# A weights-stationary last feed-forward part, later turns in the first one, and an expert path written as a loop

## The chip, the cores and the metric

The kernel runs on one core of one Trainium2 chip. The metric is the device time of one execution in microseconds (us); the figure shown for a kernel is the median of its runs. TensorE (PE) multiplies, VectorE (DVE) and ScalarE (ACT) work element-wise, GpSimd (POOL) does small work, SyncE (SP) issues the loads.

## What is computed

Two transformer blocks over 256 tokens of width 1024, all in float32. The first block is: short convolution mixer, SwiGLU feed-forward part of width 2816, latent attention, and a mixture of 8 experts of width 2048 with the top 2 per token. The second block is: two attentions side by side, then a feed-forward part of width 4096 with a squared ReLU. The parts that the change touches:

```python
def swiglu(h, w_gate, w_up, w_down):              # first feed-forward part and each expert
    return (silu(h @ w_gate) * (h @ w_up)) @ w_down

h = rmsnorm_2(x, mlp_norm_g[l])                   # last feed-forward part
u = einsum('bsd,df->bsf', h, w_up[l])
u = square(relu(u))
x = x + einsum('bsf,fd->bsd', u, w_down[l])
```

## The kernel before

**Precision.** Every float32 operand of a big product is split into a high part, which PE can take exactly, and a remainder. A product of two of them is three products on PE: high x high, remainder x high, high x remainder (`mm3`). Weights are split as they arrive (`split`, L105 to L115): ACT casts 128 x 1024 elements to `w_hi` (L113), DVE subtracts to get `w_lo` (L114). There are five buffers of each, and seven of the raw loads.

**Order.** All weights come through one stream, `weight_parts`; `get()` hands out the next split part and has one more part in the making. SP issues the loads of 1 MB in the stream's order. Tiles, semaphores and the order of each engine's instructions come from a framework that plans them when the program is built; an instruction that is not ready in that plan may let later ones pass. `behind` ties a block's instructions behind a given one, and `fence` does so for the weight splits.

**Entering a part.** `Entry` holds the normed tokens for the next part as columns: `enter` adds the result of the part before to `x` (L441), multiplies by the gain (L442), turns four 128 x 128 blocks on PE against the identity (L409), casts the high part on ACT (L410) and subtracts on DVE (L411). The row's scale `rs`, the inverse root of the mean square, is not multiplied in; it is applied to a product's rows. `half` enters the first 128 tokens while the part before still works on the second 128; `finish` enters those, and `proj` calls it after the first half's products.

**A feed-forward part** (`ffn`, L589). The hidden width is cut into chunks of 512. For each chunk `make` gives the features, and `down` multiplies the features of the chunk before into four accumulators (`acc`: two token halves, two halves of the width). In the last part `make` is `squared`: `proj` holds 128 tokens stationary and streams 512 columns of weights, 24 products for each token half; ACT applies Relu with the row scale (L1360), DVE squares (L1361), and `hidden` turns the features into columns (four transposes for each token half, L409), casts (L410) and subtracts (L411), because `down` needs them as its stationary operand. In the first part `make` is `gated`: two `proj`, Silu on ACT (L620), a product on DVE (L623), then `hidden`.

**The general expert path** (`the_rest`, L1002). The experts are worked for up to 128 tokens each. Only if one expert has more than 128 does a branch (L1006) run a body that handles the rest; the count is loaded into a register of each engine (L1005). With these inputs the branch is not taken. The body is written out for 8 experts with 4 chunks each. Behind the branch, the first instruction of PE is L960.

Of the kernel before, what the change touches and what calls it, by code (L numbers as in the profile page):

```python
# [10 lines left out]
F32 = mybir.dt.float32  # L11
# [30 lines left out]
def block_kernel(ctx: ExitStack, tc: tile.TileContext, i, out):  # L42
# [114 lines left out]
    def weight_parts():  # L157
# [45 lines left out]
        yield from up_and_down((i["w_up_2"][0],), i["w_down_2"][0])  # L203
# [137 lines left out]

    def norm(acc=None):

        hi = hts.tile([P, KD, T], F32R, tag="hT_hi", name="hT_hi")
        lo = hts.tile([P, KD, T], F32R, tag="hT_lo", name="hT_lo")
# [68 lines left out]
    class Entry:  # L414
# [5 lines left out]
        def __init__(self):  # L420
            self.h = [hts.tile([P, KD, T], F32R, tag=f"hT_{s}", name=f"hT_{s}") for s in ("hi", "lo")]
# [181 lines left out]
    def hidden(pool, made, width):  # L603
# [8 lines left out]
    with tc.tile_pool(name="parts0", bufs=2) as parts, tc.tile_pool(name="tables", bufs=1) as tp:  # L612
# [3 lines left out]
        def gated(width, first):  # L616
            pg = proj(h, width, entry.finish if first else None)
# [6 lines left out]
            a = hidden(parts, sg, width)  # L624
# [5 lines left out]
            return a  # L630
# [202 lines left out]
    with ExitStack() as moe:  # L833
# [12 lines left out]
        with tc.tile_pool(name="route", bufs=1) as rp:  # L846
# [23 lines left out]
            x_hi, x_lo = (hts.tile([P, KD, T], F32R, tag=f"hT_{s}", name=f"x_{s}") for s in ("hi", "lo"))  # L870
# [131 lines left out]
        def the_rest():  # L1002

            wg_all, wu_all, wd_all = (i[f"moe_w_{n}"][0] for n in ("gate", "up", "down"))
            n_most = nc.values_load(most_i[0:1, 0:1], min_val=0, max_val=T)  # L1005
            with tc.If(n_most > P, label="rest"):  # L1006
# [4 lines left out]
                def streamed(src):  # L1011
# [4 lines left out]
                for e in range(E):  # L1016
                    for t in range(2):
                        nc.vector.tensor_tensor(pick2[:, t], slots[:, P:T], pos[:, t, e : e + 1].to_broadcast([P, P]),
                                                op=OP.is_equal)
                    room = acts.tile([P, 2, D], F32, tag="xn", name="room", bufs=1)  # L1020
                    x2 = room[:, 0].rearrange("p (k s) -> p k s", k=KD)
                    y2 = room[:, 1]
                    b = bank()
                    for t, ts in enumerate(blocks(2)):
                        nc.tensor.transpose(b[:, ts], pick2[:, t], ident)
                    nc.vector.tensor_copy(put2, b[:, :T])
                    b = bank()
                    for t in range(2):
                        mm(b[:, 0:2], pick2[:, t], gate[:, t, e], t == 0, t == 1)
                    nc.vector.tensor_copy(g2, b[:, 0:2])  # L1030
                    for k0 in range(0, KD, 4):
                        v = bank().rearrange("p (k s) -> p k s", k=4)
                        for k in range(4):
                            ks = slice((k0 + k) * P, (k0 + k + 1) * P)
                            for t in range(2):
                                mm(v[:, k], h_hi[:, t, ks].bitcast(F32), pick2[:, t], t == 0, False)
                                mm(v[:, k], h_lo[:, t, ks].bitcast(F32), pick2[:, t], False, t == 1)
                        nc.vector.tensor_copy(x2[:, k0 : k0 + 4], v)
                    yb = [bank("yb") for _ in range(2)]
                    for c, cs in enumerate(blocks(NC, 512)):  # L1040
                        both = []
                        for w_all in (wg_all, wu_all):
                            b = bank()
                            for k, ks in enumerate(blocks(KD)):
                                mm(b, x2[:, k], streamed(w_all[e][ks, cs]), k == 0, k == KD - 1)
                            both.append(b)
                        sg = acts.tile([P, 512], F32, tag="sg", name="sg")
                        nc.scalar.activation(sg, both[0], AF.Silu, scale=g2[:, 1:2])
                        nc.vector.scalar_tensor_tensor(sg, both[1], g2[:, 1:2], sg, op0=OP.mult, op1=OP.mult)
                        bt = bank()  # L1050
                        for fs in blocks(4):
                            nc.tensor.transpose(bt[:, fs], sg[:, fs], ident)
                        a2 = parts.tile([P, 4, P], F32, tag="a_hi", name="a2")
                        nc.vector.tensor_copy(a2, bt.rearrange("p (f s) -> p f s", f=4))
                        for f in range(4):
                            for n, ns in enumerate(blocks(2, 512)):
                                mm(yb[n], a2[:, f], streamed(wd_all[e][c * 512 + f * P : c * 512 + (f + 1) * P, ns]),
                                   c + f == 0, c == NC - 1 and f == 3)
                    for n, ns in enumerate(blocks(2, 512)):
                        nc.vector.tensor_scalar(y2[:, ns], yb[n], g2[:, 0:1], None, op0=OP.mult)  # L1060
                    for t, ts in enumerate(blocks(2)):
                        for ns in blocks(2, 512):
                            b = bank()
                            mm(b, put2[:, ts], y2[:, ns], True, True)
                            nc.vector.tensor_tensor(x[:, t, ns], x[:, t, ns], b, op=OP.add)
# [288 lines left out]
    h, rs = entry.h, entry.rs  # L1354
    with tc.tile_pool(name="parts2", bufs=2) as parts:
        def squared(width, first):
            pu = proj(h, width, entry.finish if first else None)
            r = [acts.tile([P, 512], F32, tag="sg", name="sg") for _ in range(2)]
            for t in range(2):
# [57 lines left out]
```

## Time and profile before

| | |
|---|---|
| median of 3 runs | 1325.47 us (1325.12 to 1325.68) |
| the profiled execution | 1324.65 us, span 1322.9 us from first to last instruction |
| PE, weight loads | 1275.3 us (96% of the span), 1060.9 us (80%) |
| DVE, ACT | 983.5 us (74%), 807.4 us (61%) |
| mean granted TensorE clock | 0.988 of full speed |
| loads | 320.82 MB, 243 GB/s over the span |

Busy time is the sum of the instructions' records. The record of a 512-column product is some 0.39 us long and overlaps the next, so a busy PE can still have room: the start-to-start time is what counts. "Idle before, releaser" names what an instruction had waited for. The last feed-forward part lies from 1127 us to the end, the first one from 108 to 300 us, and the branch of the expert path near 415 us.

### The profile page before, as it was taken

What the parts mean: (1) busy time and instruction counts of PE and PEld (TensorE: products, weight loads), DVE (VectorE), ACT (ScalarE), POOL (GpSimd) and SP (SyncE); (2) the same over time, 40 slices, a digit from 0 to 9 for tenths busy, and PEclk for the clock granted to TensorE, in tenths of its full rate; (3) what the DMA queues carried; (4) which work ended last, traced back from release to release, by engine and by line L of the source; (5) the groups of instructions that cost most, each with busy time, mean ns of one, the idle gap of its engine ahead of it and who ended that gap; (6) DMA issues with size and microseconds to landing.
All of it is one profiled execution on the core that took longest, in us unless ns stands there. A gap on an engine that the chain in (4) does not pass through costs nothing.

```text
span 1322.9 us, 17290 instructions
## 1 busy us (share of the span) xinstructions
PE 1275.3 (96%) x6413; PEld 1060.9 (80%) x6413; DVE 983.5 (74%) x1256; ACT 807.4 (61%) x1106; POOL 82.7 (6%) x111
## 2 busy tenths in 40 slices
PE   6999999999996999999999999999998999899998
PEld 6998778888685788888888887888787986678887
DVE  6665655457856999999998888898887787655553
ACT  5444544446845877778877677777775565544442
POOL 0000201001520000000000000000001331000000
PEclk9999999999997999999999999999998999999999
DMA  9854655736425999989998898999995432455520
GB/s 315 290 177 163 228 176 126 264 112 208 163 65 203 349 364 349 373 316 356 358 357 328 324 344 324 327 342 353 340 333 178 173 100 92 162 181 176 183 95 32
DMA packets 148609, 320.82 MB, mean 243 GB/s; under 512 B 7787, under 2 KB 34438, under 8 KB 148518
## 3 DMA queue, kind: packets, MB, share of 16 engines
q1 hardware_dynamic: 142912, 314.07, 67.3%
q10 hardware_dynamic: 5606, 5.57, 1.9%
q8 instruction: 53, 0.87, 0.3%
q14 instruction: 38, 0.31, 0.1%
HBM read 317.52 MB, written 2.10 MB: 242 GB/s over the span
## 4 chain that ended last, share of the span: by engine, by line
PE 62%; DVE 3%; ACT 2%; POOL 1%; issue 1%; ACTq 0%
PE bank L58 37%; PE yb L58 13%; PE acc L58 8%; DVE w_lo L114 1%; PE bank L1105 1%; PE bank L409 1%; ACT w_hi L113 1%; PE po L58 1%; PE bank L1258 0%; POOL s L1280 0%; ACT s L1274 0%; POOL yq L1177 0%; POOL raq L1164 0%; DVE x_lo L952 0%; DVE mx L1270 0%
## 5 line engine op out<-in xcount | busy, mean ns | idle before, releaser
L114 DVE TENSOR_TENSOR w_lo<-raw,w_hi 128x1024 fp32r<-128x1024 f32 (+2 forms) x600 | 713.0, 1219 | 224.0 <-ACT w_hi L113 208.3
L113 ACT CAST w_hi<-raw 128x1024 fp32r<-128x1024 f32 (+2 forms) x600 | 608.4, 1044 | 297.9 <-PE bank L58 170.7
L58 PE MATMUL bank<-w_hi,x_hi 128*128 128x512 f32 x512 | 202.7, 396 | 0.9 <-ACT w_hi L113 0.9
L58 PE MATMUL bank<-w_lo,x_hi 128*128 128x512 f32 x512 | 201.6, 394 | 1.1 <-DVE w_lo L114 1.1
L58 PE MATMUL bank<-w_hi,x_lo 128*128 128x512 f32 x512 | 200.0, 391 | 0.0
L58 PE MATMUL bank<-w_hi,hT_hi 128*128 128x512 f32 (+1 forms) x464 | 161.8, 358 | 2.5 <-ACT w_hi L113 2.3
L58 PE MATMUL bank<-w_lo,hT_hi 128*128 128x512 f32 (+1 forms) x464 | 159.6, 354 | 1.0 <-DVE w_lo L114 0.9
L58 PE MATMUL bank<-w_hi,hT_lo 128*128 128x512 f32 (+1 forms) x464 | 159.5, 354 | 0.0
L58 PEld LDWEIGHTS bank<-w_lo,x_hi 128*128 128x128 f32 x512 | 96.4, 188 | 25.6 <-DVE w_lo L114 5.4
L58 PEld LDWEIGHTS bank<-w_hi,x_hi 128*128 128x128 f32 x512 | 96.6, 189 | 20.2 <-ACT w_hi L113 1.8
L58 PEld LDWEIGHTS bank<-w_hi,x_lo 128*128 128x128 f32 x512 | 96.5, 189 | 19.5
L58 PEld LDWEIGHTS bank<-w_hi,hT_hi 128*128 128x128 f32 x464 | 89.5, 194 | 15.3 <-ACT w_hi L113 3.4
L58 PE MATMUL yb<-w_hi,a_hi 128*128 128x512 f32 x256 | 101.1, 395 | 0.0
L58 PE MATMUL yb<-w_hi,a_lo 128*128 128x512 f32 x256 | 101.1, 395 | 0.0
L58 PEld LDWEIGHTS bank<-w_lo,hT_hi 128*128 128x128 f32 x464 | 90.0, 194 | 13.1 <-DVE w_lo L114 1.7
L58 PEld LDWEIGHTS bank<-w_hi,hT_lo 128*128 128x128 f32 x464 | 90.0, 194 | 11.4
L58 PE MATMUL yb<-w_lo,a_hi 128*128 128x512 f32 x256 | 96.4, 398 | 0.0
L58 PE MATMUL acc<-w_lo,a_hi 128*128 128x512 f32 x216 | 85.2, 394 | 0.0
L58 PE MATMUL acc<-w_hi,a_lo 128*128 128x512 f32 x216 | 85.1, 394 | 0.0
L58 PE MATMUL acc<-w_hi,a_hi 128*128 128x512 f32 x216 | 84.5, 391 | 0.0
L450 POOL TENSOR_TENSOR rs<-ms,mhalf 128x1 f32<-128x1 f32 x10 | 6.0, 598 | 835.1 <-DVE ms L449 835.1
L58 PEld LDWEIGHTS yb<-w_hi,a_lo 128*128 128x128 f32 x256 | 48.1, 188 | 11.7
(326 smaller groups left out, 1587.9 us busy)
## 6 DMA issues: line engine op xcount, KB each, us to landing
raw<-in_moe_w_gate_dram SPq DMA_DIRECT2D x64, 1024.0 KB, 6.1
raw<-in_moe_w_up_dram SPq DMA_DIRECT2D x64, 1024.0 KB, 6.7
raw<-in_moe_w_down_dram SPq DMA_DIRECT2D x64, 1024.0 KB, 6.0
raw<-in_w_up_dram SPq DMA_DIRECT2D x16, 1024.0 KB, 5.3
raw<-in_w_down_dram SPq DMA_DIRECT2D x16, 1024.0 KB, 5.0
raw<-in_conv_w_in_dram SPq DMA_DIRECT2D x12, 1024.0 KB, 13.3
raw<-in_ffn_w_gate_dram SPq DMA_DIRECT2D x11, 1024.0 KB, 5.1
raw<-in_ffn_w_up_dram SPq DMA_DIRECT2D x11, 1024.0 KB, 18.0
```

The source lines that it names most:

```text
L58: return nc.tensor.matmul(o, lhsT, rhs, start=start, stop=stop)
L113: halves[:] = [nc.scalar.copy(hv, v), nc.vector.tensor_tensor(lv, v, hv.bitcast(F32), op=OP.subtract)]
L114: nc.vector.tensor_tensor(lv, v, hv.bitcast(F32), op=OP.subtract)]
L409: nc.tensor.transpose(v[:, k], src[:, ks], ident)
L450: nc.gpsimd.tensor_tensor(self.rs[:, t : t + 1], ms, mhalf[:, :1], op=OP.pow)
L1105: nc.tensor.transpose(bt[:, fs], sg[:, fs], ident)
```

## The change

It has three parts. (1) In the last feed-forward part the weights become the stationary operand, so that the features come out as columns and need no turning. The tokens' high and remainder parts lie side by side in one tile, so that one product of 512 columns does weight-high x both; a second, of 256 columns, does weight-remainder x high. The two parts of the result lie in the two halves of a bank and are added. The row scale is positive, so relu(s u)^2 = s^2 relu(u)^2, and its square, 1/ms, is applied when the result is added to `x`. `w_up_2` is loaded by columns, 256 at a time. (2) In the first feed-forward part the turning of a chunk's features (`token_major`, before `hidden`) is handed to `ffn` as a function, which calls it in the middle of `down` of the chunk before, or, for the first chunk, in the middle of the second chunk's gate product. (3) The body of the general expert path is written once, in a loop over the 32 chunks, and adds each chunk's result to `x`.

```diff
-    def up_and_down(ups, w_down):
+    def up_and_down(ups, w_down, part=chunk_of):
...
-                yield from chunk_of(u, cs)
+                yield from part(u, cs)
...
-        yield from up_and_down((i["w_up_2"][0],), i["w_down_2"][0])
+        yield from up_and_down((i["w_up_2"][0],), i["w_down_2"][0], lambda u, cs: columns_of(u[:, cs]))
...
-    def proj(h, width, fresh=None):
+    def proj(h, width, fresh=None, midway=None):
...
         for k0 in range(0, KD, n):
+            if midway and k0 == KD // 2:
+                midway()
...
-    def down(acc, parts, first=False, last=0, done=None):
+    def down(acc, parts, first=False, last=0, done=None, midway=None):
...
-        for a, k in plain:
+        for j, (a, k) in enumerate(plain):
+            if midway and j == len(parts) // 2:
+                midway()
...
+    def h_pair(name="hT"):
+        t = hts.tile([P, KD, 2, T], F32R, tag="hT", name=name)
+        return t[:, :, 0], t[:, :, 1]
...
-            self.h = [hts.tile([P, KD, T], F32R, tag=f"hT_{s}", name=f"hT_{s}") for s in ("hi", "lo")]
+            self.both = hts.tile([P, KD, 2, T], F32R, tag="hT", name="hT")
+            self.h = self.both[:, :, 0], self.both[:, :, 1]
...
-        acc, waiting = None, []
+        acc, waiting, turn = None, [], None
         sizes = [cs.stop - cs.start for cs in chunks(n_ff)]
-        for n, size in enumerate(sizes + [0]):
-            made = make(size, n == 0) if size else None
+        parts = lambda made, size: [(made, k) for k in range(size // P)]
+        for n, size in enumerate(sizes):
+            first_turn = turn
+            turn = make(size, n == 0, (lambda: waiting.append(first_turn())) if n == 1 else None)
             if n:
                 acc = acc or new_acc()
-                down(acc, waiting, n == 1, 4 if n == len(sizes) else 0, done)
-            waiting = [(made, k) for k in range(size // P)]
+                down(acc, parts(waiting.pop(0), sizes[n - 1]), n == 1, midway=lambda: waiting.append(turn()))
+        down(acc, parts(waiting.pop(0), size), False, 4, done)
...
-        def gated(width, first):
-            pg = proj(h, width, entry.finish if first else None)
+        def gated(width, first, midway):
+            pg = proj(h, width, entry.finish if first else None, midway)
...
-            a = hidden(parts, sg, width)
...
-            return a
+            return lambda: token_major(parts, sg, width)
...
-            with tc.If(n_most > P, label="rest"):
+            with tc.If(n_most > P, label="rest"), tc.For_i(0, E * NC) as g:
+                e, c = g // NC, g % NC
...
-                for e in range(E):
...
-                    for c, cs in enumerate(blocks(NC, 512)):
...
-        def squared(width, first):
-            pu = proj(h, width, entry.finish if first else None)
-            r = [acts.tile([P, 512], F32, tag="sg", name="sg") for _ in range(2)]
-            for t in range(2):
-                nc.scalar.activation(r[t], pu[t], AF.Relu, scale=rs[:, t : t + 1])
-                nc.vector.tensor_tensor(r[t], r[t], r[t], op=OP.mult)
-            return hidden(parts, r, width)
+        def squared(width, first, midway):
+            if midway:
+                midway()
+            a = new_parts(parts, [P, 4, T])
+            for f0 in range(0, width // P, 2):
+                banks = [bank().rearrange("p (s t) -> p s t", s=2) for _ in range(2)]
+                ws = [get(), get()] if first and f0 == 0 else None
+                for ts in blocks(2) if ws else (slice(0, T),):
+                    if ts.start:
+                        entry.finish()
+                    for f, o in enumerate(banks):
+                        hi, lo = ws[f] if ws else get()
+                        for k in range(KD):
+                            mm(o[:, :, ts], hi[:, k], entry.both[:, k, :, ts], k == 0, False)
+                        for k in range(KD):
+                            mm(o[:, 0, ts], lo[:, k], entry.h[0][:, k, ts], False, k == KD - 1)
+                r = acts.tile([P, 2, T], F32, tag="sg", name="r")
+                for f, o in enumerate(banks):
+                    nc.scalar.copy(r[:, f], o[:, 1])
+                    nc.vector.tensor_tensor(r[:, f], r[:, f], o[:, 0], op=OP.add)
+                nc.vector.scalar_tensor_tensor(r, r, 0.0, r, op0=OP.max, op1=OP.mult)
+                hilo(a[0][:, f0 : f0 + 2], a[1][:, f0 : f0 + 2], r)
+            return lambda: a
 
         def store(t, acc):
+            if t == 0:
+                nc.vector.reciprocal(entry.rs, entry.ms)
             for n, ns in enumerate(blocks(2, 512)):
-                nc.vector.tensor_tensor(x[:, t, ns], x[:, t, ns], acc[n], op=OP.add)
+                nc.vector.scalar_tensor_tensor(x[:, t, ns], acc[n], entry.rs[:, t : t + 1], x[:, t, ns],
+                                               op0=OP.mult, op1=OP.add)
```

## Rows read from the trace of the kernel before

**Rows 1.** Busy time by stretch: us, PE, weight loads, DVE, ACT, POOL, clock, DMA share, GB/s.
```profile
60.00:80.00 20.00, 20.00 (x169) 20.00 (x169) 12.41 (x17) 8.38 (x9) 0.00 (x0) 1.00 0.52 161
1127.00:1160.00 33.00, 28.05 (x124) 21.65 (x123) 21.77 (x26) 17.93 (x24) 1.04 (x2) 0.95 0.57 191
1182.00:1296.00 114.00, 113.95 (x519) 93.26 (x517) 61.40 (x60) 52.77 (x61) 0.00 (x0) 1.00 0.44 148
```
**Rows 2.** PE in order of time, last part, first chunk: start, us, instruction, [idle before].
```profile
1130.02 1.98 PE L58 MATMUL bank<-w_lo,hT_hi 128*128 128x512 f32 x8
1131.84 1.98 PE L58 MATMUL bank<-w_hi,hT_lo 128*128 128x512 f32 x8
...
1140.09 0.60 PE L409 MATMUL bank<-ident,sg 128*128 128x128 f32 x4
...
1143.03 0.66 PE L409 MATMUL bank<-ident,sg 128*128 128x128 f32 x4 [2.34 <-DVE sg L1361]
1143.44 0.47 PE L58 MATMUL bank<-w_hi,hT_hi 128*128 128x512 f32 x1
```
**Rows 3.** PE in order of time, last part, second chunk.
```profile
1155.80 0.39 PE L58 MATMUL bank<-w_lo,hT_hi 128*128 128x512 f32 x1
...
1159.38 0.47 PE L58 MATMUL acc<-w_hi,a_hi 128*128 128x512 f32 x1
```
**Rows 4.** PE in order of time, last part, fourth chunk.
```profile
1204.18 0.39 PE L58 MATMUL acc<-w_hi,a_hi 128*128 128x512 f32 x1
...
1205.28 0.39 PE L58 MATMUL acc<-w_lo,a_hi 128*128 128x512 f32 x1
...
1207.35 0.60 PE L409 MATMUL bank<-ident,sg 128*128 128x128 f32 x4
...
1208.01 0.39 PE L58 MATMUL acc<-w_hi,a_hi 128*128 128x512 f32 x1
```
**Rows 5.** PE in order of time, first mixer, weights stationary.
```profile
61.50 1.12 PE L58 MATMUL bank<-hT_hi,w_lo 128*128 128x256 f32 x8
62.46 1.12 PE L58 MATMUL bank<-hT_hi,w_hi 128*128 128x256 f32 x8
```
**Rows 6.** DVE in order of time, start of the last part.
```profile
1127.59 4.62 DVE L114 TENSOR_TENSOR w_lo<-raw,w_hi 128x1024 fp32r<-128x1024 f32 x4
1132.12 0.68 DVE L441 TENSOR_TENSOR x<-x,acc 128x512 f32<-128x512 f32 x1
```
**Rows 7.** Groups of instructions: count, then busy us, mean ns, idle before.
```profile
L1361 DVE TENSOR_TENSOR sg<-sg 128x512 f32<-128x512 f32 x16 | 11.0, 688 | 0.5 <-ACT sg L1360 0.5
...
L410 ACT CAST a_hi<-bank 128x512 fp32r<-128x512 f32 x26 | 15.1, 582 | 11.0 <-DMA g_k<-in_mla_k_norm_dram 8.8 <-PE bank L409 2.1
```
**Rows 8.** DVE in order of time, a 256-column step from a bank.
```profile
1111.49 0.42 DVE L1329 TENSOR_TENSOR mb<-po,rsb 128x256 f32<-128x256 f32 x1 [0.88 <-POOL rsb L1328]
```
**Rows 9.** ACT in order of time, a 256-column cast from a bank.
```profile
421.38 0.37 ACT L963 CAST put<-bank 128x256 fp32r<-128x256 f32 x1 [6.26 <-PE bank L58]
```
**Rows 10.** PE in order of time, first feed-forward part, first chunk's second turn.
```profile
132.68 0.66 PE L409 MATMUL bank<-ident,sg 128*128 128x128 f32 x4 [0.48 <-DVE sg L623]
```
**Rows 11.** The branch's line by queue: count, ns (least, median, most), first and last start.
```profile
L1006 SPq EVENT_SEMAPHORE  x8: 17/17/17, 419.1 to 419.7; - x8
...
L1006 ACTq COMPARE_BRANCH  x1: 62/62/62, 413.3 to 413.3; - x1
L1006 ACTq EVENT_SEMAPHORE  x1: 17/17/17, 413.8 to 413.8; - x1
...
L1006 DVEq COMPARE_BRANCH  x1: 72/72/72, 417.3 to 417.3; - x1
L1006 DVEq EVENT_SEMAPHORE  x1: 21/21/21, 419.9 to 419.9; - x1
```
**Rows 12.** DVE in order of time, its last work ahead of the branch.
```profile
416.90 1.22 DVE L114 TENSOR_TENSOR w_lo<-raw,w_hi 128x1024 fp32r<-128x1024 f32 x1
```
**Rows 13.** PE in order of time, its first instruction behind the branch.
```profile
420.04 0.66 PE L960 MATMUL bank<-ident,pick 128*128 128x128 f32 x2 [5.05 <-DVEq L1006]
```

More of the change, by code (lines that the diff above doesn't have):

```diff
@@ L589, in ffn, with token_major @@
     def ffn(n_ff, make, done):
-        acc, waiting = None, []
+        acc, waiting, turn = None, [], None
         sizes = [cs.stop - cs.start for cs in chunks(n_ff)]
-        for n, size in enumerate(sizes + [0]):
-            made = make(size, n == 0) if size else None
+        parts = lambda made, size: [(made, k) for k in range(size // P)]
+        for n, size in enumerate(sizes):
+            first_turn = turn
+            turn = make(size, n == 0, (lambda: waiting.append(first_turn())) if n == 1 else None)
             if n:
                 acc = acc or new_acc()
-                down(acc, waiting, n == 1, 4 if n == len(sizes) else 0, done)
-            waiting = [(made, k) for k in range(size // P)]
+                down(acc, parts(waiting.pop(0), sizes[n - 1]), n == 1, midway=lambda: waiting.append(turn()))
+        down(acc, parts(waiting.pop(0), size), False, 4, done)
     def new_parts(pool, shape):
         return [pool.tile(shape, F32R, name=f"a_{s}") for s in ("hi", "lo")]
-    def hidden(pool, made, width):
+    def token_major(pool, made, width):
         n = width // P
@@ L869, in block_kernel @@
                     mm(lT, wide_r[:, k], h[s][:, k], s + k == 0, s == 1 and k == KD - 1)
-            x_hi, x_lo = (hts.tile([P, KD, T], F32R, tag=f"hT_{s}", name=f"x_{s}") for s in ("hi", "lo"))
+            x_hi, x_lo = h_pair("xT")
             lT_sb = rp.tile([2 * E, T], F32, name="lT_sb")
@@ L1002, in the_rest @@
         def the_rest():
-            wg_all, wu_all, wd_all = (i[f"moe_w_{n}"][0] for n in ("gate", "up", "down"))
+            wg_all, wu_all = (i[f"moe_w_{n}"][0] for n in ("gate", "up"))
+            wd_all = i["moe_w_down"][0].rearrange("e f d -> (e f) d")
             n_most = nc.values_load(most_i[0:1, 0:1], min_val=0, max_val=T)
-            with tc.If(n_most > P, label="rest"):
+            with tc.If(n_most > P, label="rest"), tc.For_i(0, E * NC) as g:
+                e, c = g // NC, g % NC
                 pick2 = ep.tile([P, 2, P], F32, tag="pick", name="pick2", bufs=2)
@@ L1014, in streamed @@
                     return w
-                for e in range(E):
-                    for t in range(2):
[L1018 to L1022, printed above, removed]
-                    b = bank()
[L1024 to L1039, printed above, removed]
-                    for c, cs in enumerate(blocks(NC, 512)):
[L1041 to L1058, printed above, removed]
-                    for n, ns in enumerate(blocks(2, 512)):
[L1060 to L1065, printed above, removed]
@@ new lines, in the_rest @@
+                for t in range(2):
+                    nc.vector.tensor_tensor(pick2[:, t], slots[:, P:T],
+                                            pos[:, t, bass.ds(e, 1)].to_broadcast([P, P]), op=OP.is_equal)
+                room = acts.tile([P, 2, D], F32, tag="xn", name="room", bufs=1)
+                x2 = room[:, 0].rearrange("p (k s) -> p k s", k=KD)
+                y2 = room[:, 1]
+                b = bank()
+                for t, ts in enumerate(blocks(2)):
+                    nc.tensor.transpose(b[:, ts], pick2[:, t], ident)
@@ new lines, in the_rest @@
+                nc.vector.tensor_copy(put2, b[:, :T])
+                ge = ep.tile([P, 2, 1, 2], F32, tag="ge", name="ge", bufs=1)
+                nc.vector.tensor_copy(ge, gate[:, :, bass.ds(e, 1)])
+                b = bank()
+                for t in range(2):
+                    mm(b[:, 0:2], pick2[:, t], ge[:, t, 0], t == 0, t == 1)
+                nc.vector.tensor_copy(g2, b[:, 0:2])
+                for k0 in range(0, KD, 4):
+                    v = bank().rearrange("p (k s) -> p k s", k=4)
+                    for k in range(4):
+                        ks = slice((k0 + k) * P, (k0 + k + 1) * P)
+                        for t in range(2):
+                            mm(v[:, k], h_hi[:, t, ks].bitcast(F32), pick2[:, t], t == 0, False)
+                            mm(v[:, k], h_lo[:, t, ks].bitcast(F32), pick2[:, t], False, t == 1)
+                    nc.vector.tensor_copy(x2[:, k0 : k0 + 4], v)
@@ new lines, in the_rest @@
+                both = []
+                for w_all in (wg_all, wu_all):
+                    b = bank()
+                    for k, ks in enumerate(blocks(KD)):
+                        w = streamed(w_all[bass.ds(e, 1), ks, bass.ds(c * 512, 512)].rearrange("e p f -> p (e f)"), k)
+                        mm(b, x2[:, k], w, k == 0, k == KD - 1)
+                    both.append(b)
+                sg = acts.tile([P, 512], F32, tag="sg", name="sg")
+                nc.scalar.activation(sg, both[0], AF.Silu, scale=g2[:, 1:2])
@@ new lines, in the_rest @@
+                nc.vector.scalar_tensor_tensor(sg, both[1], g2[:, 1:2], sg, op0=OP.mult, op1=OP.mult)
+                bt = bank()
+                for fs in blocks(4):
+                    nc.tensor.transpose(bt[:, fs], sg[:, fs], ident)
+                a2 = parts.tile([P, 4, P], F32, tag="a_hi", name="a2")
+                nc.vector.tensor_copy(a2, bt.rearrange("p (f s) -> p f s", f=4))
+                yb = [bank("yb") for _ in range(2)]
+                for f in range(4):
+                    for n, ns in enumerate(blocks(2, 512)):
+                        mm(yb[n], a2[:, f], streamed(wd_all[bass.ds(g * 512 + f * P, P), ns], f), f == 0, f == 3)
@@ L1067, in block_kernel @@
+                for n, ns in enumerate(blocks(2, 512)):
+                    nc.vector.tensor_scalar(y2[:, ns], yb[n], g2[:, 0:1], None, op0=OP.mult)
+                for t, ts in enumerate(blocks(2)):
+                    for ns in blocks(2, 512):
+                        b = bank()
+                        mm(b, put2[:, ts], y2[:, ns], True, True)
+                        nc.vector.tensor_tensor(x[:, t, ns], x[:, t, ns], b, op=OP.add)
         tc.mark_branch_hint_location("rest")
```

7 lines of the change are left out of this document (2 added, 5 removed).

## The prediction

> **What bounds the kernel now.** I first read busy time by stretch [rows 1]. TensorE (PE) is busy 113.95 of 114.00 us in the body of the last feed-forward part, ACT and DVE about half of it, and the DMA engines 0.44: PE's stream sets this stage, so a gain must be PE time. The same view shows where PE is not full: 28.05 of the 33 us from 1127 to 1160, with the granted clock at 0.95. Next I read PE in order of time, to see what stands between the products. A 512-column product takes 0.2275 us from start to start (eight in 1.82 us, [rows 2]), so the 768 products of the last feed-forward part need 174.7 us by themselves. What PE's rows show between those products is all that the change can win there, and the working goes through it chunk by chunk.
>
> **What goes.** The turning of the features into columns (64 transposes in 16 groups of four), the waits in front of them, and what the waits do to the clock.
> - First chunk: the first group starts at 1140.09 when the products are over, the second waits 2.34 us for the square on DVE, and the next product starts at 1143.44 [rows 2]: 3.35 us.
> - The clock behind it: 0.95 of 2.4 GHz over 33 us [rows 1] means 3.3 us at 1.2 GHz, in which half the work was lost: 33 x 0.05 = 1.65 us.
> - Second chunk: last product at 1155.80 + 0.23, next one at 1159.38 [rows 3]: 3.35 us.
> - Chunks three to eight: here the groups already stand amid other products. From 1204.18 to 1205.28 lie two products (0.455) and one group: 0.645 us. From 1207.35 to 1208.01 lie a group and one product: 0.43 us [rows 4]. 1.08 us a chunk, six chunks: 6.45 us.
> Sum 14.8 us. A reader who takes the 16 groups as 16 waits would claim far more; only the first two chunks wait.
>
> **What comes in its place.** Per feature block, 8 products of 512 columns (high part of the weights against both token parts) and 8 of 256 (low part): 256 + 256 instructions for 384. Products of 256 columns with the weights stationary stand in the first mixer: eight in 0.96 us, 0.12 each [rows 5]. 256 x 0.2275 + 256 x 0.12 = 88.96 us against 384 x 0.2275 = 87.36: +1.6 us.
> The first pair of blocks is done token half by token half: 32 products of 256 columns and 32 of 128 for 16 of 512 and 16 of 256 (5.56 us). The trace has no such 128-column product with a new weight each; bounds are half of 0.12 (the column share) and 0.12 (nothing saved), so 5.8 to 7.7 us. I take 0.09, the middle: 6.7 us, +1.2 us (0.2 to 2.1).
> The rule against the narrow products is in the Trainium skill, "TensorE: Matmul & The Clock Gate", section "LDWEIGHTS (loading the stationary operand)": a load of 128 columns takes 128/1.2 = 107 ns, as long as 256 columns stream. By it the 128-column products cost 0.107 each, 7.3 us for the pair; the traced 0.12 for 256 columns agrees that such a product is not yet much slowed by its load.
>
> **Entry of the stage.** The second token half enters (add, gain, transposes, cast, remainder) under the products of the first. These were 24 x 0.2275 = 5.46 us and become 16 x 0.12 + 16 x 0.09 = 3.4 us: 2.1 us less cover. The side-by-side product also wants the remainders of the tokens at once, one DVE step of some 0.69 us later (as wide as the square, [rows 7]). Against it, DVE now does four weight remainders (4.62 us) before it adds the last quarter of the second half at 1132.12 [rows 6]; two parts are fetched here where there were four, so that quarter can enter up to 2.3 us earlier. Best case 0; worst 2.1 + 0.7 and another stretch of half clock like the one above, 1.65: 4.5. I take +1.5 us, since an order made anew seldom takes all that it could.
>
> **ACT and DVE.** Per chunk of 512 features DVE gives up two squares (0.688, [rows 7]) and gets four adds of 256 columns (nearest row 0.42, [rows 8]) and two 512-wide max-and-multiply steps, which read and write as the square does (0.688); the remainders stay: +1.7 us a chunk. DVE was busy 61.4 of 114 us [rows 1], 12 of 22 us a chunk; 13.9 of 22 still leaves PE the bound. ACT swaps two Relu of 512 columns for four copies of 256 (nearest row 0.37, [rows 9]): the same number of elements, and +1.5 us a chunk even if Relu had cost nothing, on an engine busy 52.8 of 114. Both hide under 22 us of products; with no cover the +1.7 would be 13.6 us in all. The row scale that moves to the end makes DVE's last step a scaled add, for which I allow 0.1 us at the tail; the reciprocal's input is ready long before.
>
> **Loads.** w_up comes as rows of 1 KB instead of 2 KB, same sixteen issues on SP, same order. The first mixer reads 1 KB rows: 161 GB/s at 0.52 of the DMA engines, so some 310 at full load, against 148 needed here [rows 1]. Cost nothing; without that margin the load would bind. The Trainium skill, "Perfetto Trace Analysis", section "DMA Optimizations", says transfers under 2 KB pay a large overhead each; 0.52/161 against 0.44/148 shows 9% more engine time per byte, where PE is the bound.
>
> **First feed-forward part.** Moving its turns to the middle of other products keeps the 1.08 us a chunk and can only remove waits; the largest is 0.48 us in the first chunk [rows 10]. Turns and casts move behind the next gate weights' splits and behind the table DMAs that ACT issues. What PE wins there it may lose at the next weights, because those splits wait on ACT too. I take -0.3 us (-1 to +1).
>
> **The general expert path.** Its branch is not taken, so its body costs only the jump over it. DVE's branch at 417.3 takes 0.07 us, but its next instruction, the semaphore that releases PE [rows 13], comes at 419.9, 2.5 us after the branch [rows 11]; the work that DVE had before it ends at 416.90 + 1.22 = 418.12 [rows 12]. ACT, which has little code in that path, goes from branch to next instruction in about half a microsecond [rows 11]. So about 1.7 us of PE's 5.05 us wait [rows 13] is the jump over DVE's long body. The body written once as a loop is a thirty-second of the unrolled chunks: I take -1.7 us. Bounds: all engines may have to meet where a loop's counts are reset. SP runs its last semaphore of the branch at 419.7 [rows 11]; a meeting starts there, and if it takes a few times ACT's half microsecond, PE is released up to 2 us later than now: +2. If PE no longer waits for DVE at all, it could go at about 417: -3.
> The Trainium skill, "Runtime: NRT & Kernel Launch", section "Instruction fetch mechanics", says a jump out of the fetched window must wait for its code; by it the 1.7 us would go whole. That fits DVE's 2.5 against ACT's half.
>
> **Sum.** -14.8 + 1.6 + 1.2 + 1.5 - 0.3 - 1.7 + 0.1 (tail) = -12.4 us. The profiled execution took 1324.65 us (span 1322.9), so 1312.2; the median of the runs is 0.8 higher: 1313.
>
> **Rivals.**
> 1. *The stage's start eats it.* Entry at its worst (4.5 for 1.5), narrow products at 0.12 (+0.9), a meeting at the branch (+2 for -1.7), first part +1: -3.6 us, 1318 to 1322. For it: 1127 to 1160 is already the weakest stretch [rows 1]. Against: all of it must come together; one alone leaves 1315 to 1317. Chance 0.15.
> 2. *The jump pays more.* Wait down to 2 us, and with it the half clock behind it: 1305 to 1309. Chance 0.08.
> 3. *Slower: weights wait behind the new element-wise chain.* After a pair's last product come copy 0.37, add 0.42, max-and-multiply 0.69, cast 0.58, remainder 0.69: 2.75 us on ACT and DVE in turn [rows 7 to 9]. Were the next weight's remainder (1.22, [rows 12]) queued behind it on DVE, it would be ready after 4.0 us, where PE has one weight's 2.78 us of products in hand: 1.2 us lost in each of 16 pairs, 19 us: 1332. PE waits then, and its banks and the next copies behind it. It decides from 12.4 / 16 = 0.8 us a pair on. Against: PE's only long waits now are for features, not weights, and ACT is less than half busy [rows 1]. Chance 0.07.
> 4. *No difference,* 1322.8 to 1328.1 (0.2% is about what a measurement of this kernel can tell from none): turns were hidden anyway. PE's rows speak against: they stand in PE's own stream [rows 4]. Chance 0.06.
> The forecast, 1309 to 1318, has 0.64.
>
> **Numbers.** Faster 0.64 + 0.15 + 0.08 = 0.87, lowered to 0.86 for rival 1's edge; same 0.07; slower 0.07. Range 1306 to 1321, which leaves out rival 3, rival 4 and the ends of the other two.
>
> **What would show it.** No transposes of features in the last stage; its PE stretch from 1127 shorter by some 10 us, and at full clock; pairs of blocks at 5.56 us; PE's wait at the branch near 3.4 us. Wrong if PE waits for weight parts in that stage, if the wait for the second token half passes 4 us, or if the wait at the branch grows.

## The result and the profile after

The kernel after takes 1311.11 us (median of 4 runs, 1310.36 to 1311.97) against 1325.30 us before (4 runs, 1324.14 to 1325.68): ratio 0.9895, 95% interval 0.9877 to 0.9912, 14.2 us less. The forecast was 1313.0 us.

The two profiled executions stand 12.7 us apart (spans 1310.2 and 1322.9 us). Cut at products that both kernels have, TensorE's stream shows where:

| stretch (start of first to start of last product) | before, us | after, us | change | forecast |
|---|---|---|---|---|
| span's start to first mixer's last product | 108.18 | 109.25 | +1.07 | 0 |
| on to the gather's last group of products | 304.15 | 302.94 | -1.21 | -0.3 |
| on to the first expert's first product (the branch) | 8.87 | 6.82 | -2.05 | -1.7 |
| experts and second mixer, to its last product | 705.57 | 705.70 | +0.13 | 0 |
| last feed-forward part, to its last product | 191.77 | 181.04 | -10.73 | -10.5 |
| on to the span's end | 4.36 | 4.45 | +0.09 | +0.1 |

The +1.07 arises before 23.2 us, in the first loads and the first products behind them, ahead of anything that the change is meant to touch, and belongs to the execution: between profiled executions of the experiments below this place lies anywhere from 107.4 to 109.1. Of the -1.21 some 0.2 is the clock of the gather's products and not the change; the other 1.0 lies in the first feed-forward part.

Busy time by stretch, kernel after, the 33 us around the start of the last part and 114 us of its body, in the columns of [rows 1]:
```profile
1125.00:1158.00 33.00, 31.59 (x196) 28.05 (x195) 26.72 (x36) 19.76 (x30) 0.97 (x2) 1.00 0.57 192
1180.00:1294.00 114.00, 114.00 (x579) 97.28 (x578) 70.75 (x82) 54.16 (x72) 0.00 (x0) 1.00 0.43 139
```
The first stretch went from 28.05 us of PE at a clock of 0.95 to 31.59 at 1.00. In the body PE is still the bound, DVE rose from 61.40 to 70.75 us and ACT from 52.77 to 54.16: hidden work, as the prediction put it.

PE in order of time, kernel after, from the second mixer's last product over the first pair of blocks:
```profile
1124.71 0.40 PE L58 MATMUL acc<-w_lo,m_hi 128*128 128x512 f32 x1
1124.94 1.63 PE L58 MATMUL bank<-hT,w_hi 128*128 128x256 f32 x11
1126.41 1.01 PE L58 MATMUL bank<-hT,w_lo 128*128 128x128 f32 x8
1127.26 0.81 PE L58 MATMUL bank<-hT,w_hi 128*128 128x256 f32 x5
...
1128.75 1.15 PE L417 MATMUL bank<-ident,xg 128*128 128x128 f32 x8
1131.31 1.46 PE L58 MATMUL bank<-hT,w_hi 128*128 128x256 f32 x10 [1.41 <-DVE hT L419]
...
1135.06 2.07 PE L58 MATMUL bank<-hT,w_hi 128*128 128x512 f32 x8
```
Read starts, not durations: eight 128-column products take 1127.26 - 1126.41 = 0.85 us, 0.106 each. The pair lasts 10.12 us (1124.94 to 1135.06): 7.23 of products (32 x 0.12 + 32 x 0.106) and 2.89 of entry, of which PE waits 1.41 for the tokens. The view of waits of PE from 1125 us to the last product has only that one row, of 1.4 us, and none for weights.

The same view in the body: the pairs of blocks of one chunk, between the starts of two successive down projections.
```profile
1173.93 0.40 PE L58 MATMUL acc<-w_hi,a_hi 128*128 128x512 f32 x1
...
1184.83 1.98 PE L58 MATMUL bank<-hT,w_hi 128*128 128x512 f32 x8
1186.65 1.12 PE L58 MATMUL bank<-hT,w_lo 128*128 128x256 f32 x8
1187.60 2.00 PE L58 MATMUL bank<-hT,w_hi 128*128 128x512 f32 x8
1189.44 1.11 PE L58 MATMUL bank<-hT,w_lo 128*128 128x256 f32 x8
1190.39 1.78 PE L58 MATMUL bank<-hT,w_hi 128*128 128x512 f32 x7
...
1195.98 0.40 PE L58 MATMUL acc<-w_hi,a_hi 128*128 128x512 f32 x1
```
A pair takes 1190.39 - 1184.83 = 5.56 us, as forecast, and a chunk 1195.98 - 1173.93 = 22.05 us; before, the last five such steps took 22.89 to 22.94. No transpose stands between.

The branch's line by queue, kernel after, columns of [rows 11]:
```profile
L1018 PEldq COMPARE_BRANCH  x1: 352/352/352, 412.8 to 412.8; - x1
...
L1018 DVEq COMPARE_BRANCH  x1: 72/72/72, 416.9 to 416.9; - x1
L1018 DVEq EVENT_SEMAPHORE  x1: 21/21/21, 418.1 to 418.1; - x1
```
DVE's semaphore came 2.5 us after its branch [rows 11], 1.7 us after the work queued ahead of it had ended. It comes 1.2 us after it now, as soon as that work ends (a 1.22 us remainder that starts at 416.83). PE goes on at 418.25 instead of 420.04 [rows 13].

### The profile page after: what moved, and what is told of

Read it like the earlier page. It is cut to its first block, busy times and chain, and to the rows that moved or that the text cites. A ratio compares the mean times of both kernels' runs of the same rounds, so it can differ in the third digit from the quotient of the medians.

```text
span 1310.2 us, 17521 instructions
## 1 busy us (share of the span) xinstructions
PE 1266.7 (97%) x6509; PEld 1063.8 (81%) x6509; DVE 995.5 (76%) x1289; ACT 804.3 (61%) x1121; POOL 76.6 (6%) x111
## 4 chain that ended last, share of the span: by engine, by line
PE 61%; DVE 3%; ACT 2%; issue 1%; POOL 1%; DMA 0%; POOLq 0%; ACTq 0%
PE bank L58 38%; PE yb L58 13%; PE acc L58 8%; DVE w_lo L114 1%; PE bank L1118 1%; ACT w_hi L113 1%; PE po L58 0%; DMA raw<-in_moe_w_up_dram 0%; POOL s L1293 0%; PE bank L1271 0%; PE bank L417 0%; DVE mx L1283 0%; ACT s L1287 0%; POOL yq L1190 0%; POOL raq L1177 0%
## 5 line engine op out<-in xcount | busy, mean ns | idle before, releaser
L58 PE MATMUL bank<-w_hi,xT 128*128 128x512 f32 x1024 | 319.8, 393 | 0.9 <-ACT w_hi L113 0.9
L58 PEld LDWEIGHTS bank<-w_hi,xT 128*128 128x128 f32 x1024 | 191.0, 189 | 39.7 <-ACT w_hi L113 1.7
L58 PE MATMUL bank<-w_lo,xT 128*128 128x512 f32 x512 | 201.4, 393 | 1.1 <-DVE w_lo L114 1.1
L58 PE MATMUL bank<-w_hi,hT 128*128 128x256 f32 (+1 forms) x672 | 164.8, 340 | 3.2 <-ACT w_hi L113 2.9
L58 PEld LDWEIGHTS bank<-w_hi,hT 128*128 128x128 f32 x672 | 118.1, 195 | 16.6 <-ACT w_hi L113 3.4
L58 PE MATMUL bank<-hT,w_hi 128*128 128x256 f32 (+1 forms) x656 | 115.8, 325 | 1.4 <-DVE hT L419 1.4
L58 PEld LDWEIGHTS bank<-w_lo,xT 128*128 128x128 f32 x512 | 96.4, 188 | 25.5 <-DVE w_lo L114 5.3
L58 PE MATMUL bank<-w_lo,hT 128*128 128x256 f32 (+1 forms) x336 | 111.5, 339 | 1.1 <-DVE w_lo L114 0.9
L58 PEld LDWEIGHTS bank<-hT,w_hi 128*128 128x128 f32 x656 | 96.4, 192 | 10.2 <-DVE hT L419 1.6
L58 PEld LDWEIGHTS bank<-w_lo,hT 128*128 128x128 f32 x336 | 65.7, 196 | 8.0 <-DVE w_lo L114 1.7
L58 PEld LDWEIGHTS yb<-w_hi,a_hi 128*128 128x128 f32 x256 | 48.1, 188 | 11.5
L58 PEld LDWEIGHTS yb<-w_hi,a_lo 128*128 128x128 f32 x256 | 48.1, 188 | 11.5
```

The costliest lines, as they stand in the source:

```text
L58: return nc.tensor.matmul(o, lhsT, rhs, start=start, stop=stop)
```

## The experiments

The loop, the short body and the late turns are edits of the kernel before, the dearer features, the entries and the early branch edits of the kernel after. Ratios are to the kernel before, run on the same chip.

**The loop alone, and a short body without a loop.**
```
-                for e in range(E):                  # inside the branch
+ (loop alone)   with tc.If(...), tc.For_i(0, E * NC) as g:
+ (short body)   for e in range(1):
```


> The kernel before with the general expert path written as a loop, and nothing else changed. Theory (the jump over a long body is what is saved): faster by 1.7 us as predicted, and by what the trace after shows at that place up to 2.3 us; PE's wait for DVE after the branch falls from 5.05 to about 4.0 us and PE's own branch from 4.28 to about 0.35 us. Rival (the loop's counts make all engines meet): slower by up to 2 us, PE's wait 5 to 7 us. Third possibility (the gain at that place in the trace after belongs to another part of the change): no change within 0.5 us.

> The kernel before, where the general expert path, which is not taken, is written for one expert instead of eight, still unrolled, with no loop (seven of the eight experts of that path are left out). It tells the length of the body from the loop. Theory (what is saved is the jump over a long body): the same gain as with the loop alone, 1.7 to 2.3 us, PE's wait after the branch near 4.0 us. If the time goes with the length in proportion, a body four times that of the loop gives a little less, 1.5 to 2.0 us. Rival (the gain comes from how a loop leaves the engines' semaphores and not from length): no gain, PE's wait near 5 us.

Loop: 1323.72 us (11 runs, 1320.54 to 1325.04) against 1324.95 (27 runs), ratio 0.9984 (0.9975 to 0.9994), which is 2.1 us with an interval from 0.8 to 3.3. Short body: 1324.22 us (11 runs), ratio 0.9995 (0.9986 to 1.0004), 0.7 us, which by itself could be nothing, or 1.7. The traces tell more. The branch's line by queue and PE's next instruction, loop alone:
```profile
L1007 PEldq COMPARE_BRANCH  x1: 352/352/352, 413.3 to 413.3; - x1
...
L1007 DVEq COMPARE_BRANCH  x1: 72/72/72, 417.9 to 417.9; - x1
L1007 DVEq EVENT_SEMAPHORE  x1: 21/21/21, 418.8 to 418.8; - x1
```
```profile
418.92 0.66 PE L960 MATMUL bank<-ident,pick 128*128 128x128 f32 x2 [3.29 <-DVEq L1007]
```
The same two views, short body:
```profile
L1006 PEldq COMPARE_BRANCH  x1: 4061/4061/4061, 413.7 to 413.7; - x1
...
L1006 DVEq COMPARE_BRANCH  x1: 72/72/72, 418.3 to 418.3; - x1
L1006 DVEq EVENT_SEMAPHORE  x1: 21/21/21, 419.1 to 419.1; - x1
```
```profile
419.27 0.66 PE L960 MATMUL bank<-ident,pick 128*128 128x128 f32 x2 [3.04 <-DVEq L1006]
```
With an eighth of the body and no loop, DVE's semaphore comes 0.8 us after its branch, as with the loop; in both that is just the end of the 1.22 us remainder queued ahead (it starts at 417.84 here, at 417.49 with the loop), so nothing of DVE's jump is left to be paid. PE's own branch still takes 4.06 us, to 417.7, against this in the kernel before:
```profile
L1006 PEldq COMPARE_BRANCH  x1: 4281/4281/4281, 412.7 to 412.7; - x1
```
PE's wait falls to 3.0 all the same: PE's own jump was hidden under DVE's queue, and only DVE's jump was paid. So the length of the body is what counts, and the loop's meeting costs nothing here: from the gather's last group to the first expert product the loop takes 7.16 us and the short body 7.15, against 8.87 before (8.87 to 9.07 in the four traces that write out all eight experts and branch behind the gather).

The loop's profiled execution is no shorter as a whole (span 1323.0 us against 1322.9), though it gains these 1.7 us at the branch: its last part took 193.2 us instead of 191.8. Busy time by stretch there:
```profile
1127.00:1160.00 33.00, 28.10 (x122) 22.03 (x120) 21.15 (x25) 16.94 (x23) 0.56 (x1) 0.92 0.57 192
```
The clock is 0.92 where [rows 1] have 0.95, in code that is the same. So the kernel before varies by over a microsecond with how often PE's clock falls behind the two long waits of its last part, and the span of one profiled run is no measure of a 1.7 us edit. That the loop gains is shown by the rows of the branch and by the interval of its runs; how much of it arrives, 1.2 us by the medians and 2.1 by the ratio, the runs leave open.

**Late turns in the first feed-forward part alone.**
```
+    turn = make(size, n == 0, ...)           # returns a function that turns
+    down(..., midway=lambda: waiting.append(turn()))
```


> The kernel before with the turning of the features moved amid other products in the first feed-forward part alone; the last part still turns at once. Predicted -0.3 us (-1 to +1); the trace after shows about -0.95 us over the first two chunks and nothing in the later ones. Theory (only the waits of the first chunks are removed): faster by 0.3 to 1.0 us. Rival (turning late also frees PE time in every chunk, two parts of which the trace hides): 2 us or more faster. Rival (late turns put casts ahead of the next weights): 0.5 us or more slower, with new waits of PE for weights in that part.

1323.92 us (11 runs) against 1324.95, ratio 0.9993 (0.9984 to 1.0002): the runs cannot tell it from no change. In the trace the first down projection starts 1.05 us earlier than before, counted from the end of the first mixer, and the rest of the part takes as long as before though it holds one turn more (one stands ahead of that point now, two stood there before). This repeats: the part's last down product starts 191.6 to 191.8 us after the mixer's last product in four traces that turn at once, and 190.5 to 190.7 us after it in four that turn late. PE in order of time:
```profile
134.63 1.04 PE L413 MATMUL bank<-ident,sg 128*128 128x128 f32 x8
136.49 0.50 PE L58 MATMUL bank<-w_hi,hT_hi 128*128 128x512 f32 x1 [0.82 <-ACT w_hi L113]
```
The eight transposes stand together and the 0.48 us wait for the product [rows 10] is gone, but PE then waits 0.82 us for the next weights, whose cast queues on ACT. That trade was named in the prediction, and the first chunk wins nothing by it. The gain comes from the chunks behind: eight transposes in one group cost 0.80 us and some 0.1 at the product after them, against about 1.1 for two groups set between products (the 1.08 of [rows 4]).

**The last part alone.** The kernel after without the loop and with the first part turning at once.

> The kernel before with the last feed-forward part alone changed: weights stationary, both token parts side by side, no turning; the first part turns at once and the general expert path is unrolled as before. Theory (the last part alone carries the gain): faster by 10.5 us (9.5 to 11.5), its stretch from the end of the first mixer's last products as in the kernel after, PE at full clock from 1127 on, 5.2 to 5.5 us of it in the first two chunks and 5.3 us in the other six. Rival (the parts help each other, so that alone they are worth less): less than 9 us.

1313.48 us (4 runs) against 1324.95, ratio 0.9915 (0.9900 to 0.9930): 11.5 us, the upper end of what was expected. Its last part takes 181.06 us, the kernel after 181.04, so the other two edits do nothing to this one. The three medians sum to 1.2 + 1.0 + 11.5 = 13.7 us of the 14.2; two of them are uncertain by about their own size, and the stretches of the traces are the better sum: 10.7 in the last part, 1.7 at the branch, 1.0 in the first part.

**Late turns in both parts, products as before.**
```
     def squared(width, first, midway):
+        pu = proj(h, width, ..., midway)
-        return hidden(parts, r, width)
+        return lambda: hidden(parts, r, width)
```


> The kernel before with the turning moved amid other products in both feed-forward parts: the last part keeps its products and its turning and only does it later, in every chunk. Theory (in the last part the waits and the clock of the first two chunks make 3.35 + 3.35 + 1.65 us less the turning itself, 2 x 1.08 us, and the other six chunks only pay the turning): faster by 5 to 7 us, 0.3 to 1 us of it in the first part; of the full change's 10.5 us in the last part some 4 to 5 are then left for the new order of the products. Rival (the half clock there comes from the entry of the second token half and not from the waits for turning): faster by 3 to 5 us. Rival (the last part's gain is all the turning's own time): 1 us or less.

1316.33 us (5 runs) against 1325.73, ratio 0.9928 (0.9915 to 0.9942): 9.4 us, more than I expected. Its last part takes 183.53 us, 8.24 less than before and only 2.5 more than the kernel after. Busy time by stretch, then PE in order of time:
```profile
1128.00:1161.00 33.00, 32.54 (x154) 26.14 (x153) 23.94 (x27) 20.64 (x27) 1.56 (x2) 1.00 0.58 201
```
```profile
1158.86 1.04 PE L413 MATMUL bank<-ident,sg 128*128 128x128 f32 x8
1159.65 0.48 PE L58 MATMUL acc<-w_hi,a_hi 128*128 128x512 f32 x1
...
1204.21 1.03 PE L413 MATMUL bank<-ident,sg 128*128 128x128 f32 x8
1205.00 0.48 PE L58 MATMUL acc<-w_hi,a_hi 128*128 128x512 f32 x1
```
PE no longer waits for a turn, and the clock stays at 1.00 though the entry is the one of before: the half clock in [rows 1] came with the waits for the turn, not with the entry. The eight transposes in one group, with the gaps around them, cost 0.83 us a chunk (22.67 us a chunk less 96 x 0.2275), not the 1.08 of [rows 4]: my expectation left out this 0.25 us in six chunks, 1.5 us. The first two chunks give 3.35 + 3.35 + 1.65 - 2 x 0.83 = 6.7 us; together 8.2. The side-by-side products then earn the rest: 8 x 0.83 = 6.6 us of turning gone, 1.6 for the 256-column products, 1.7 for the narrow ones and 0.7 at the entry paid, 2.6 us by this sum.

**Dearer features.**
```
-  scalar_tensor_tensor(r, r, 0.0, r, max, mult)
+  tensor_scalar(r, r, 0.0, max); tensor_tensor(r, r, r, mult)
+  tensor_tensor(r, r, r, max);   tensor_tensor(r, r, r, max)
```


> The kernel after with the maximum and the product of the features done in four steps on DVE instead of one, three steps of 0.69 us more in every pair of blocks, 16 pairs, with the same values. Theory (the element-wise chain of the last part lies under the products, DVE at some 14 of 22 us a chunk): no change within 0.5 us though DVE gets 33 us more work; at most the first chunk's products wait. Rival (the weights wait behind that chain, as in the forecast's third rival): slower by up to 16 x 2.07 = 33 us, and 10 us or more if only half the pairs wait.

1311.47 us (4 runs), ratio 0.9892 (0.9877 to 0.9907), as the kernel after. Busy time by stretch, its body:
```profile
1180.00:1294.00 114.00, 114.00 (x578) 97.31 (x577) 87.27 (x113) 54.09 (x72) 0.00 (x0) 1.00 0.43 138
```
DVE went from 70.75 to 87.27 us and PE's row did not move; chunks stay at 22.05 us. The third rival, weights waiting behind the element-wise chain, is refuted: DVE took 16.5 us more in the 10.3 pairs of this stretch, 1.6 us a pair, and no product came later.

**The entry: no halves, high products alone in halves, one remainder later, and the kernel after again.**
```
no halves:        if first and f0 == 0: entry.finish()      # before any product
high halves:      high(o, w, slice(0, P))                   # 16 products, 256 columns
                  entry.finish(); <put-off remainders>
                  high(o, w, slice(P, T)); low(o, w)        # low ones undivided
remainder later:  <third block's remainder issued behind entry.finish()>
```


> The kernel after without the division of the first pair of blocks by token halves: the second half enters before any product of the last part. Theory (the narrow products pay for themselves by covering the entry): the narrow products cost 0.106 each, so dropping them gives 1.7 us back, but PE then waits for the whole entry, some 5 us instead of 1.4, and its clock falls: slower by 2 to 4 us. Rival (the division costs more than it covers): faster by 0.5 to 1.5 us.

> The kernel after, where only the high products of the first pair of blocks are done token half by token half (256 columns each), the low products behind the entry at their full width, and the weight remainders of the next two blocks put behind the entry's steps on DVE. Theory (the entry can be covered cheaply: 16 products of 256 columns, 1.92 us, at an extra price of some 0.2 us, where the narrow products of the kernel after cost 1.7 and the remainders ahead of the last quarter hold the entry up): the stretch from the last product of the second mixer to the first of the down projection is 1.5 to 2.5 us shorter than in the kernel after (27.16 us there, 26.65 without any division). Rival (put off, the remainders come too late and PE waits for weights instead): no gain or a loss against the kernel after.

> The kernel after with one change: the weight remainder of the third block (1.2 us on DVE), which stands ahead of the entry's last quarter, is put behind the entry. Theory (PE's wait of 1.41 us at the entry is DVE still doing weight remainders): that wait falls by 0.9 to 1.2 us and the stretch to the first down product with it, 26.0 to 26.3 us. Rival (the wait is the length of the entry's own chain, add, gain, turning, cast, remainder): the wait stays within 0.3 us of 1.41.

> The kernel after once more, on the chip of the two variants of its entry, so that they can be compared with it. 1311 us, within 1.5 us; the stretch from the last product of the second mixer to the first of the down projection 27.2 us as in its first trace.

| kernel | median, us (4 runs) | ratio (interval) | last product before to first down product, us |
|---|---|---|---|
| after | 1311.11 | 0.9895 (0.9877 to 0.9912) | 27.16 |
| after again | 1311.42 | 0.9903 (0.9887 to 0.9920) | 27.18 |
| no halves | 1311.09 | 0.9891 (0.9876 to 0.9906) | 26.65 |
| remainder later | 1310.79 | 0.9893 (0.9877 to 0.9910) | 26.61 |
| high halves | 1310.03 | 0.9890 (0.9873 to 0.9906) | 25.53 |

No halves, PE in order of time, up to the second pair:
```profile
1126.37 0.63 PE L417 MATMUL bank<-ident,xg 128*128 128x128 f32 x4 [2.09 <-DVE ms L458]
1126.75 1.17 PE L58 MATMUL bank<-hT,w_hi 128*128 128x512 f32 x4
1128.40 1.20 PE L58 MATMUL bank<-hT,w_hi 128*128 128x512 f32 x4 [0.48 <-DVE hT L419]
```
I expected a loss of 2 to 4 us here and found a gain of 0.5 in this stretch, and no difference that the medians can tell. PE waits 2.57 us instead of 1.41 and its clock stays at 1.00; the narrow products cost 1.7 us to save less than that. So by this stretch the division does not pay in the kernel after.

One remainder later, PE's wait and the DVE rows that hold it up:
```profile
1131.16 1.45 PE L58 MATMUL bank<-hT,w_hi 128*128 128x256 f32 x10 [0.96 <-DVE hT L427]
```
```profile
1127.05 0.68 DVE L458 TENSOR_TENSOR x<-x,acc 128x512 f32<-128x512 f32 x1
1127.64 1.22 DVE L115 TENSOR_TENSOR w_lo<-raw,w_hi 128x1024 fp32r<-128x1024 f32 x1
1128.78 0.68 DVE L459 TENSOR_TENSOR xg<-x,gain 128x512 f32<-128x512 f32 x1
```
The remainder moved behind one step of the entry and not behind all of it, and the wait fell by 0.45 us: half of what I expected, in the direction of the theory that remainders on DVE hold the entry up. How much of the other 0.96 us is the entry's own chain stays open.

High halves, PE in order of time:
```profile
1124.47 2.25 PE L58 MATMUL bank<-hT,w_hi 128*128 128x256 f32 x16
1126.56 0.60 PE L425 MATMUL bank<-ident,xg 128*128 128x128 f32 x4
1127.53 0.66 PE L425 MATMUL bank<-ident,xg 128*128 128x128 f32 x4 [0.37 <-DVE xg L459]
1128.56 1.22 PE L58 MATMUL bank<-hT,w_hi 128*128 128x256 f32 x8 [0.37 <-DVE ms L466]
1130.04 0.74 PE L58 MATMUL bank<-hT,w_hi 128*128 128x256 f32 x4 [0.26 <-DVE hT L427]
```
Three short waits of 1.0 us in all, no narrow product, and 1.63 us less in this stretch than the kernel after, as expected; the edit makes two changes at once, and no run parts the wider products from the put-off remainders. On the same chip its four runs (1309.38 to 1310.22) lie below all four of the kernel after (1311.28 to 1312.31): it beats both kernels, by 1.4 us over the one after.

**The branch ahead of the gather.**
```
+ the_rest()
  gather(pick)
- the_rest()
```


> The kernel after with the branch of the general expert path placed ahead of the gathering products of the first expert instead of behind them. Theory (with a short body PE's branch costs 0.35 us, and what PE then waits for, DVE's work up to 418.1, is the same in either order): no change to 1 us faster, since the gathering products can then fill PE's wait for DVE. Rival (the branch makes every engine wait for the value that decides it, and the gathering products no longer hide this): slower by 1 to 4 us.

1314.47 us (5 runs) against 1325.73, ratio 0.9920 (0.9907 to 0.9934): some 3 us slower than the kernel after. The branch's line by queue, and PE:
```profile
L1018 DVEq COMPARE_BRANCH  x1: 72/72/72, 416.3 to 416.3; - x1
L1018 DVEq EVENT_SEMAPHORE  x1: 21/21/21, 416.9 to 416.9; - x1
```
```profile
417.06 1.20 PE L58 MATMUL bank<-pick,h_hi 128*128 128x256 f32 x4 [10.08 <-DVEq L1018]
```
DVE reaches the branch at nearly the same time in either order (416.3 us here, 416.9 in the kernel after), behind its own queue of remainders and gate steps. The gather's products used to run under this; now they wait for it. My theory fell, the rival holds.

## Why the prediction was right

The mechanism was right, and the sum came out by its own steps, in part because errors of opposite sign cancelled.

- *What goes, 14.8 us.* Confirmed: the late turns alone got back the two waits and the clock, and the chunk period of before is the 21.84 + 1.08 = 22.92 of the working.
- *256-column products, +1.6.* The chunk takes 22.05 us against 21.84 for its products before: 0.21 x 8 = 1.7.
- *Narrow products, +1.2.* Mis-sized: 0.106 each, not 0.09, so +1.7, inside the stated bounds. The Trainium skill, "TensorE: Matmul & The Clock Gate", section "LDWEIGHTS (loading the stationary operand)", puts a load's time in ns at its columns divided by 1.2, by which 128 columns take 107 ns, an estimate; the trace agrees, with 0.106 us from start to start over the eight (a single load's record is longer, 0.19 us, and overlaps the next).
- *Entry, +1.5.* Measured +0.7 (2.89 us beside the products, against 13.08 - 48 x 0.2275 = 2.16 in the first chunk of before, from its first product at 1127.01 to its first turn at 1140.09). The fear of another half clock was unfounded, the clock row shows 1.00. The errors of this term and of the narrow products offset, which is luck: -10.5 forecast for the last part, -10.73 measured.
- *First part, -0.3.* About -1.0 by the traces, the edge of its range; the runs alone cannot confirm it. The step that fell short is the 1.08 us a chunk that was kept for turning: in one group of eight it costs some 0.2 us less, in every chunk.
- *Branch, -1.7.* -1.7 by the traces of the two runs that change it alone, -2.05 in the first trace of the kernel after. The second trace of that kernel has 7.16 us there again, -1.7. With a short or looped body behind the gather, traces with a mean granted clock of 0.71 to 0.72 over the gather's products have 6.58 to 6.82 us there, those with 0.56 to 0.60 have 7.15 to 7.16, so the odd 0.35 goes with the clock. The reading that DVE's jump sets it, and not PE's longer one, is shown by the short body. PE's wait was to be near 3.4: 3.29 and 3.04 alone, 3.99 in the kernel after, where PE finished the gather sooner and so began to wait earlier. The Trainium skill, "Runtime: NRT & Kernel Launch", section "Instruction fetch mechanics", says a branch out of the fetched window stalls for its code. The runs agree in that a long body costs DVE 1.7 us and a body of one expert nothing that shows, while PE's branch stays long over that one (4.06 us); no run here shows the fetching itself.
- *ACT, DVE and loads at nothing.* Shown by the dearer features (DVE) and by the absence of any wait of PE for weights or for what ACT makes.

The measured median is 1.9 us below the forecast: 0.7 from the first part, 0.2 in the last part, and the remaining 1.0 is within what executions differ by. One sum of the prediction is off by 0.1: its first rival's terms give -3.5 us, not -3.6, which changes nothing in its bounds.

## What to carry to other kernels

Before rearranging products to be rid of a turn, try turning later: that alone gave 8.2 of the last part's 10.7 us, because the waits and the lost clock were the larger part of it and the transposes the smaller. Cover for a late entry should be made of products that lose little by being narrow, and what another engine can do later should not be queued ahead of the entry. Code that is not run still cost its jump here on the engine that passed the branch last, and shortening it on another engine (PE, 4.06 to 0.35 us) gained nothing more. An edit worth a microsecond is better read from the stretch that it touches than from a span in which the clock falls once more or less.

## What the runs showed of the hardware that was not expected

- PE's branch over the unrolled body takes 4.28 us (3.45 to 4.28 in four traces), over an eighth of it still 4.06, over the loop 0.35; it is no price by length.
- Products of 128 columns with a new weight each go every 0.106 us, hardly below the 0.12 of 256 columns.
- A wait of 2.34 us was followed by half clock (1.2 of 2.4 GHz) in the kernel before and not in the trace of the late turns in the first part alone, though its last part is the same code. In that trace the clock fell behind the second chunk's wait of 1.91 us, behind which the kernel before kept full clock; the loop's and the short body's traces saw it fall behind both. A wait of 2.09 us at the entry without halves was not followed by half clock. What decides it stays open.

Busy time by stretch, late turns in the first part alone, behind the first wait and behind the second:
```profile
1143.00:1153.00 10.00, 10.00 (x47) 8.32 (x46) 6.13 (x7) 4.25 (x6) 0.00 (x0) 1.00 0.87 298
1158.00:1161.00 3.00, 3.00 (x8) 2.33 (x8) 0.69 (x1) 0.35 (x1) 0.00 (x0) 0.50 0.00 0
```
